# High and low halves of the activations and weights stored woven into one another

## The chip, the core and the metric

The kernel runs on one core of a Trainium2 chip. Five engines matter here: TensorE (PE in the profile, with its loads of the stationary operand shown apart as PEld), VectorE (DVE), ScalarE (ACT), GpSimd (POOL, nearly idle) and SyncE (SP), whose queue issues the transfers. The metric is the device time of one execution in microseconds (us), lower is better.

## What is computed

One decoder layer over 256 tokens of width 4096, in float32: two large products (4096 x 12288 and 4096 x 4096), between them attention over 16 heads and a causal pooling mixer, and around them a modulated normalisation.

```python
c_act = jax.nn.silu(c)
mod = c_act @ w_ada[l] + b_ada[l]
shift, scale, gate = jnp.split(mod, 3, axis=-1)
h = rmsnorm(x, norm_gain[l])
h = h * (1.0 + scale[:, None, :]) + shift[:, None, :]
proj = jnp.einsum('bsd,dn->bsn', h, w_in[l])
q, k, v, g_attn, u_pool, g_pool = jnp.split(proj, ...)
y_attn = longnet_mixture(q, k, v).reshape(B, S, D_ATTN) * jax.nn.silu(g_attn)
y_pool = multiscale_pool(u_pool, w_pool[l], pool_scale[l]) * jax.nn.silu(g_pool)
y = jnp.concatenate([y_attn, y_pool], axis=-1) @ w_out[l]
x = x + gate[:, None, :] * y
return rmsnorm(x, final_gain)
```

## The kernel before

A float32 product is made of three faster ones. Each operand is split into a high half, which ScalarE writes by a cast to the type float32r (4 bytes an element), and a low half, the rounded remainder, which VectorE writes by a subtraction. TensorE then adds high x high, high x low and low x high in PSUM.

Weights come in pieces. `split_piece` (L228) fetches 2 x 128 rows by 512 columns (512 KB) into a tile `raw` (7 buffers), ScalarE casts it into `wh` (L237), VectorE writes the remainder `wl` (L238); `wh` and `wl` have three buffers each. `products` (L241) issues the 12 products of a piece (L248): 2 row tiles x 2 token halves, first the eight that read `wh` as the moving operand (512 columns), against high and low activations in turn, then the four that read `wl`. The stationary operand, 128 x 128, is a token half of the activations: `hh` or `hl` for `w_in`, `yh` or `yl` (tiles named `sa`) for `w_out`.

The activations `hh` and `hl` are made 2 of 32 row tiles at a time by `build_h` (L203): a modulation vector, summed up by VectorE out of `w_ada` (L161), gives scale and bias, ScalarE applies them (`hf`, L221) and casts `hh` (L223), VectorE subtracts to give `hl` (L224). There are 16 such units; five buffers of each tile go round among them (`WIN`).

The work is interleaved by hand: `visit` (L276) walks a chunk of 512 output columns over the activations that are ready, `tick` runs the hooks that make the next modulation vector, and partial sums go to SBUF (L289, L291). The attention and the pooling (`pool_mix`, whose `lin` at L510 reads pieces of `w_pool` as the stationary operand, L522 to L524) run between visits; the gates (L161 on `gacc`) and the chunks of `w_out` (`out_chunk`, L630) come last. The last six pieces of the last chunk are kept in spare tiles so that the second token half can be done apart (L614). Each engine works its queue in program order.

Of the kernel before, what the change touches and what calls it, by code (L numbers as in the profile page):

```python
# [7 lines left out]
F32 = mybir.dt.float32  # L8
F32R = mybir.dt.float32r
AF = mybir.ActivationFunctionType  # L10
ALU = mybir.AluOpType
AX = mybir.AxisListType

P = 128
S = 256
NT = S // P
D = 4096
KT = D // P
CH = 512
# [10 lines left out]
HB = 2  # L30
# [11 lines left out]
PIECE = 2  # L42
# [3 lines left out]
WHB = 3  # L46
WLB = 3
PSB = 2
PSMB = 4
LINE = 512  # L50
RAW = PIECE * CH
# [4 lines left out]
def tile_hybrid_block(  # L56
# [17 lines left out]
    nc = tc.nc  # L74
# [4 lines left out]
    strm = ctx.enter_context(tc.tile_pool(name="strm", bufs=2))  # L79

    def slot_a(shape, dtype=F32):
        return accp.tile(shape, dtype, name="sa", bufs=16, align_bytes=LINE)

    def slot_b(shape, dtype=F32):
        return accp.tile(shape, dtype, name="sb", bufs=8, align_bytes=LINE)
# [4 lines left out]
    def misc():  # L90
        return ps_m.tile([P, CH], F32, name="psm")

    def raw_tile():
        return strm.tile([P, RAW], F32, name="raw", bufs=RAWB)
# [32 lines left out]
    pt = misc()  # L127
# [44 lines left out]
    def flush_work():  # L172
        while delayed:
            delayed.pop(0)()
# [25 lines left out]
    hs = {}  # L200
    htile = {}

    def build_h(u, acc, pool, xT):  # L203
        flush_work()
        uk, k0 = UNITS[u], US[u]
        pc = misc()
        for j in range(2 * uk):
            nc.tensor.matmul(pc[:, j:j + 1], lhsT=acc[:, j * P:(j + 1) * P], rhs=ones, start=True, stop=True)  # L208
        s12 = const.tile([P, 2, HB], F32, name="s12", bufs=2)
        ks = slice(k0, k0 + uk)  # L210
        nc.vector.tensor_tensor(out=s12[:, 0, 0:uk], in0=pc[:, 0:uk], in1=colB[:, ks], op=ALU.add)
        nc.vector.tensor_tensor(out=s12[:, 1, 0:uk], in0=pc[:, uk:2 * uk], in1=gainc[:, ks], op=ALU.mult)
        nc.vector.tensor_tensor(out=s12[:, 1, 0:uk], in0=s12[:, 1, 0:uk], in1=gb[:, ks], op=ALU.add)  # L213
        for a in range(0, uk, 2):
            kk = k0 + a
            if kk % HB == 0:
                htile[kk // HB] = [pool.tile([P, HB, S], F32R, name=n, align_bytes=LINE) for n in ("hh", "hl")]
            hh, hl = [v[:, kk % HB:kk % HB + 2] for v in htile[kk // HB]]
            hf = strm.tile([P, 2, S], F32, name="hf")
            for i in range(2):  # L220
                nc.scalar.activation(out=hf[:, i], in_=xT[:, kk + i], func=AF.Identity,  # L221
                                     scale=s12[:, 1, a + i:a + i + 1], bias=s12[:, 0, a + i:a + i + 1])
            nc.scalar.copy(out=hh, in_=hf)  # L223
            nc.vector.tensor_tensor(out=hl, in0=hf, in1=hh.bitcast(F32), op=ALU.subtract)  # L224
            for i in range(2):
                hs[kk + i] = (hh[:, i], hl[:, i])

    def split_piece(src, n, spare=False):  # L228
        rt = raw_tile()
        v = rt.rearrange("p (k n) -> p k n", n=CH)  # L230
        nc.sync.dma_start(out=v[:, 0:n], in_=src)
        if spare:
            wh, wl = [slot_a([P, PIECE, CH], F32R) for _ in range(2)]
        else:
            wh = strm.tile([P, PIECE, CH], F32R, name="wh", bufs=WHB, align_bytes=LINE)
            wl = strm.tile([P, PIECE, CH], F32R, name="wl", bufs=WLB, align_bytes=LINE)
        nc.scalar.copy(out=wh[:, 0:n], in_=v[:, 0:n])  # L237
        nc.vector.tensor_tensor(out=wl[:, 0:n], in0=v[:, 0:n], in1=wh[:, 0:n].bitcast(F32), op=ALU.subtract)  # L238
        return wh, wl

    def products(pt, hv, wh, wl, first, last):  # L241
        n = len(hv)
        seq = [(t, i, p, wh) for i in range(n) for t in range(NT) for p in range(2)]
        seq += [(t, i, 0, wl) for t in range(NT) for i in range(n)]
        for e, (t, i, p, w) in enumerate(seq):
            started = first and not any(q[0] == t for q in seq[:e])
            ended = last and not any(q[0] == t for q in seq[e + 1:])
            nc.tensor.matmul(pt[t], lhsT=hv[i][p][:, t * P:(t + 1) * P], rhs=w[:, i], start=started, stop=ended)  # L248

    chains = []  # L250
    pending = []
# [2 lines left out]
    def tick(n):  # L254
        for f in hooks:
            f(n)
        for ch in list(chains):
            ch.pop(0)()
            if not ch:
                chains.remove(ch)  # L260
        if pending and len(chains) < DEPTH and not (chains and pending[0][0] == "alone"):
            ch = pending.pop(0)
            if ch[0] == "alone":
                ch.pop(0)
            ch.pop(0)()
            if ch:
                chains.append(ch)
# [76 lines left out]
    for u in range(A0):  # L344
        build_h(u, first[u][0][0], hp, xT)
# [50 lines left out]
    yh = [None] * 8  # L396
    yl = [None] * 8
# [186 lines left out]
    for c, ch in enumerate(order):  # L584
# [5 lines left out]
        elif 12 <= ch < 16:  # L590
            i = ch - 12
# [13 lines left out]
    def need_gate(n):  # L605
        while len(gate_q) > GPS * (7 - n):
            gate_q.pop(0)()

    def prods_of_tile(pt, t, pieces, last):
        seq = []  # L610
        for hv, wh, wl in pieces:
            seq += [(hv[i][p], w[:, i]) for i in range(len(hv)) for p, w in ((0, wh), (1, wh), (0, wl))]
        for e, (h, w) in enumerate(seq):
            nc.tensor.matmul(pt[t], lhsT=h[:, t * P:(t + 1) * P], rhs=w, start=False,  # L614
                             stop=last and e == len(seq) - 1)

    def finish(t, fg):
# [12 lines left out]
    def out_chunk(n):  # L630
        cs = slice(n * CH, (n + 1) * CH)
        if n < 7:
            pw = ps.tile([P, NT, CH], F32, name="mm")
            pt = [pw[:, t] for t in range(NT)]
        else:
            pt = [misc() for t in range(NT)]
        xn.append(slot_b([P, NT, CH]))
        nc.sync.dma_start(out=xn[n], in_=x_v[:, :, cs])
        fg = fin.tile([P, CH], F32, name="fg")
        nc.sync.dma_start(out=fg, in_=fg_v[:, cs].to_broadcast([P, CH]))  # L640
        k = 0
        held = []
        while k < KT:
            m = min(PIECE, KT - k)
            if k + 2 * PIECE >= KT > k + PIECE:
                need_gate(n)
            wh, wl = split_piece(wo_v[:, k:k + m, cs], m, n == 7 and KT - HELD * PIECE <= k < KT - SPARE * PIECE)
            while not all(ydone[kk // HG] == HG for kk in range(k, k + m)):
                tick(0)
            yv = [(yh[kk // 4][:, kk % 4], yl[kk // 4][:, kk % 4]) for kk in range(k, k + m)]  # L650
            if n == 7 and k + m > KT - HELD * PIECE:
                held.append((yv, wh, wl))
                prods_of_tile(pt, 0, held[-1:], k + m == KT)
            else:
                products(pt, yv, wh, wl, k == 0, k + m == KT)
            k += m
            tick(m)
        xc = xn[n]
        gt = gates[n]
        y = fin.tile([P, NT, CH], F32, name="yo")  # L660

        def close(tp):
            w = [P, tp.stop - tp.start, CH]
            src = pw if n < 7 else pt[tp.start].unsqueeze(1)
            nc.vector.tensor_tensor(out=y[:, tp], in0=src, in1=gt.unsqueeze(1).to_broadcast(w), op=ALU.mult)
            nc.vector.tensor_tensor(out=xc[:, tp], in0=y[:, tp], in1=xc[:, tp], op=ALU.add)
            for t in range(tp.start, tp.stop):
                nc.scalar.activation(out=y[:, t], in_=xc[:, t], func=AF.Square, accum_out=ss2[:, t, n:n + 1])

        if n < 7:  # L670
            close(slice(0, NT))
            nc.vector.tensor_tensor(out=xc, in0=xc, in1=fg.unsqueeze(1).to_broadcast([P, NT, CH]), op=ALU.mult)
        else:
            nc.scalar.activation(out=r2, in_=ss2[:, :, 6], func=AF.Sqrt)
            for t in range(NT):
                if t > 0:
                    prods_of_tile(pt, t, held, True)
                close(slice(t, t + 1))
                finish(t, fg)

    for n in range(8):
        out_chunk(n)
# [54 lines left out]
```

## Time and profile before

| | before |
|---|---|
| time, median of 2 runs | 1568.45 us (1568.26 to 1568.64) |
| the profiled execution: its time, its span | 1567.34 us, 1565.4 us |
| PE busy in the span | 1516.3 us, 97% |
| DVE busy | 1405.4 us, 90% |
| ACT busy | 697.6 us, 45% |
| granted TensorE clock | 0.997 of full speed |
| share of PE in the chain that ended last | 91%, 83% in L248 alone |

A group of instructions is read as: line, engine, operation, what it writes and reads, shapes, count, then busy us and mean ns of one, then the idle time of its engine before it and who ended it. Matmuls overlap, so the mean of one is longer than the step from one to the next; the step is read off the start times of a timeline, or from the chain of work, where a stretch of products has its length and its count.

### The profile page before, as it was taken

The numbers are of one execution on the slowest core, as the hardware profiler recorded it, in microseconds if no ns is written. First come the engines' busy times: TensorE is split into PE (matmuls) and PEld (weight loads), VectorE is DVE, ScalarE is ACT, GpSimd is POOL, SyncE is SP. The second block draws the span as 40 slices with busy tenths as digits, with TensorE's granted clock in tenths as the row PEclk, the third lists the DMA queues.
The fourth block names the chain that finished last, engine by engine and source line by source line (L and its number), as shares of the span: only waits on it lengthen the run. The fifth ranks groups of instructions, "written<-read, shape, count | busy, mean of one in ns | idle before, by whom it ended". The sixth has DMA issues, their size and how long they took to land.

```text
span 1565.4 us, 20360 instructions
## 1 busy us (share of the span) xinstructions
PE 1516.3 (97%) x7043; PEld 1257.5 (80%) x7043; DVE 1405.4 (90%) x1759; ACT 697.6 (45%) x820; POOL 0.7 (0%) x5
## 2 busy tenths in 40 slices
PE   2999999999999999999999999999999999999997
PEld 2877888888888888888888888888898888888775
DVE  5988999999999998899999998989988788898886
ACT  4655344443443434344344344556554443444433
POOL 0000000000000000000000000000000000000000
PEclk9999999999999999999999999999999999999999
DMA  9999999999999999899999998867778899998886
GB/s 331 363 335 362 321 331 321 324 308 336 327 310 327 312 330 313 294 326 326 354 340 331 330 333 307 290 226 242 231 250 273 287 357 347 318 339 324 320 305 250
DMA packets 324087, 491.11 MB, mean 314 GB/s; under 512 B 19320, under 2 KB 150664, under 8 KB 323984
## 3 DMA queue, kind: packets, MB, share of 16 engines
q1 hardware_dynamic: 323984, 489.82, 92.2%
q8 instruction: 55, 0.90, 0.2%
q14 instruction: 48, 0.39, 0.1%
HBM read 485.55 MB, written 4.19 MB: 313 GB/s over the span
## 4 chain that ended last, share of the span: by engine, by line
PE 91%; DVE 3%; DMA 3%; issue 1%; ACT 1%; SPq 0%; DVEq 0%; ACTq 0%
PE mm L248 83%; DVE aacc L161 1%; PE psm L614 1%; PE psm L248 1%; DMA raw<-in_w_ada_dram 1%; DMA raw<-in_w_in_dram 1%; PE psm L208 1%; DVE wl L238 1%; ACT wh L237 1%; PE psm L523 0%; PE psm L524 0%; PE psm L522 0%; DMA sb<-in_x_dram 0%; DMA raw<-in_w_out_dram 0%; PE psm L565 0%
## 5 line engine op out<-in xcount | busy, mean ns | idle before, releaser
L237 ACT CAST wh<-raw 128x1024 fp32r<-128x1024 f32 x514 | 538.5, 1050 | 700.0 <-PE mm L248 497.9
L238 DVE TENSOR_TENSOR wl<-raw,wh 128x1024 fp32r<-128x1024 f32 x514 | 624.5, 1218 | 45.1 <-ACT wh L237 41.9
L248 PE MATMUL mm<-wh,hh 128*128 128x512 f32 x1536 | 605.4, 394 | 4.8 <-ACT wh L237 3.8
L248 PE MATMUL mm<-wh,hl 128*128 128x512 f32 x1536 | 599.6, 390 | 0.0
L248 PE MATMUL mm<-wl,hh 128*128 128x512 f32 x1536 | 414.2, 391 | 0.6 <-DVE wl L238 0.6
L161 DVE SCALAR_TENSOR_TENSOR aacc<-raw,cact,aacc 128x512 f32<-128x512 f32 x496 | 371.0, 748 | 31.4 <-DMA raw<-in_w_ada_dram 23.8
L248 PEld LDWEIGHTS mm<-wh,hh 128*128 128x128 f32 x1536 | 288.8, 188 | 67.0 <-ACT wh L237 7.2
L248 PEld LDWEIGHTS mm<-wl,hh 128*128 128x128 f32 x1536 | 288.4, 188 | 61.1 <-DVE wl L238 1.4
L248 PEld LDWEIGHTS mm<-wh,hl 128*128 128x128 f32 x1536 | 288.9, 188 | 58.3 <-issue 0.2
L248 PE MATMUL mm<-wh,sa 128*128 128x512 f32 x896 | 224.0, 392 | 1.9 <-ACT wh L237 1.9
L248 PEld LDWEIGHTS mm<-wh,sa 128*128 128x128 f32 x896 | 167.7, 188 | 39.7 <-ACT wh L237 3.4
L161 DVE SCALAR_TENSOR_TENSOR gacc<-raw,cact,gacc 128x512 f32<-128x512 f32 x248 | 185.5, 748 | 13.5 <-DMA raw<-in_w_ada_dram 9.8
L248 PE MATMUL mm<-wl,sa 128*128 128x512 f32 x448 | 119.8, 389 | 0.0
L291 DVE TENSOR_TENSOR sa<-mm,sa 128x1024 f32<-128x1024 f32 x92 | 112.1, 1218 | 8.5 <-PE mm L248 8.4
L248 PEld LDWEIGHTS mm<-wl,sa 128*128 128x128 f32 x448 | 84.0, 188 | 17.5
L291 DVE TENSOR_TENSOR sb<-mm,sb 128x1024 f32<-128x1024 f32 x48 | 58.5, 1219 | 7.3 <-PE mm L248 7.3
L328 PE MATMUL psm<-diag_r,sb 128*128 128x128 f32 x128 | 16.9, 300 | 15.9 <-DVE diag_r L320 15.9
L221 ACT ACTIVATE hf<-xT,s 128x256 f32<-128x256 f32 x32 | 17.5, 595 | 27.9 <-DVE s L213 27.9
L328 PEld LDWEIGHTS psm<-diag_r,sb 128*128 128x128 f32 x128 | 16.6, 215 | 16.1 <-DVE diag_r L320 16.1
L289 ACT COPY sa<-mm 128x1024 f32<-128x1024 f32 x16 | 16.3, 1016 | 14.2 <-PE mm L248 14.1
L248 PE MATMUL psm<-wh,sa 128*128 128x512 f32 x80 | 20.1, 394 | 1.4 <-ACT wh L237 1.4
L248 PEld LDWEIGHTS psm<-wh,sa 128*128 128x128 f32 x80 | 14.8, 188 | 5.3 <-ACT wh L237 2.2
(113 smaller groups left out, 618.1 us busy)
## 6 DMA issues: line engine op xcount, KB each, us to landing
raw<-in_w_in_dram SPq DMA_DIRECT2D x384, 512.0 KB, 5.7
raw<-in_w_ada_dram SPq DMA_DIRECT2D x512, 256.0 KB, 5.3
raw<-in_w_ada_dram SPq DMA_DIRECT2D x128, 512.0 KB, 6.5
raw<-in_w_out_dram SPq DMA_DIRECT2D x128, 512.0 KB, 6.8
sb<-in_x_dram SPq DMA_DIRECT2D x16, 512.0 KB, 6.4
raw<-in_w_pool_dram SPq DMA_DIRECT2D x8, 512.0 KB, 4.7
out_dram<-sb SPq DMA_DIRECT2D x16, 256.0 KB, 2.6
fg<-in_final_gain_dram SPq DMA_DIRECT2D x8, 256.0 KB, 4.7
```

The lines of the kernel that those rows point to most:

```text
L161: nc.vector.scalar_tensor_tensor(out=acc, in0=r, scalar=cact[:, kt:kt + 1], in1=init if kt == 0 else acc, op0=ALU.mult, op1=ALU.add)
L208: nc.tensor.matmul(pc[:, j:j + 1], lhsT=acc[:, j * P:(j + 1) * P], rhs=ones, start=True, stop=True)
L221: nc.scalar.activation(out=hf[:, i], in_=xT[:, kk + i], func=AF.Identity, scale=s12[:, 1, a + i:a + i + 1], bias=s12[:, 0, a + i:a + i + 1])
L237: nc.scalar.copy(out=wh[:, 0:n], in_=v[:, 0:n])
L238: nc.vector.tensor_tensor(out=wl[:, 0:n], in0=v[:, 0:n], in1=wh[:, 0:n].bitcast(F32), op=ALU.subtract)
L248: nc.tensor.matmul(pt[t], lhsT=hv[i][p][:, t * P:(t + 1) * P], rhs=w[:, i], start=started, stop=ended)
L289: nc.scalar.copy(out=accs[ch], in_=pt)
L291: nc.vector.tensor_tensor(out=accs[ch], in0=pt, in1=accs[ch], op=ALU.add)
L328: nc.tensor.matmul(px[:, i * S + t * P:i * S + (t + 1) * P], lhsT=xs[q][:, t, (2 * a + i) * P:(2 * a + i + 1) * P], rhs=diag_r[:, t], star ...
L614: nc.tensor.matmul(pt[t], lhsT=h[:, t * P:(t + 1) * P], rhs=w, start=False, stop=last and e == len(seq) - 1)
```

## The change

High and low halves get one tile for both. A piece of weights has a tile `wb` of twice the size, with three buffers, in place of `wh` and `wl`. In every other piece the halves lie one behind the other in it, as before; in the rest they are woven: high, low, high, low, so that neighbouring elements of one half are 8 bytes apart where they were 4. The activations of a unit have a tile `hb`, in one of four layouts by turns (`kind`): 0, halves apart (4 bytes between neighbours); 1, high and low woven (8 bytes); 2, both row tiles and both halves woven (16 bytes); 3, halves apart and the two token halves woven (8 bytes between the elements of one token half). The cast and the subtraction of a unit, one instruction each for both row tiles before, are now one for each row tile. `products` and `prods_of_tile` take ready slices, so no product is added, dropped or moved.

```diff
@@ build_h
-                htile[kk // HB] = [pool.tile([P, HB, S], F32R, name=n, align_bytes=LINE) for n in ("hh", "hl")]
-            hh, hl = [v[:, kk % HB:kk % HB + 2] for v in htile[kk // HB]]
+                hb = pool.tile([P, 2 * HB * S], F32R, name="hb", align_bytes=LINE)
+                kind = kk // HB % 4
+                if kind == 0:
+                    v = hb.rearrange("p (l k s) -> p k l s", l=2, k=HB)
+                elif kind == 1:
+                    v = hb.rearrange("p (k s l) -> p k l s", l=2, k=HB)
+                elif kind == 2:
+                    v = hb.rearrange("p (s k l) -> p k l s", l=2, k=HB)
+                else:
+                    v = hb.rearrange("p (k l s t) -> p k l t s", l=2, k=HB, t=NT)
+                htile[kk // HB] = (kind, v)
+            kind, v = htile[kk // HB]
+            hh, hl = [v[:, :, l] for l in range(2)]
...
-            nc.scalar.copy(out=hh, in_=hf)
-            nc.vector.tensor_tensor(out=hl, in0=hf, in1=hh.bitcast(F32), op=ALU.subtract)
+            src = hf if kind < 3 else hf.rearrange("p k (t s) -> p k t s", t=NT)
             for i in range(2):
-                hs[kk + i] = (hh[:, i], hl[:, i])
+                nc.scalar.copy(out=hh[:, i], in_=src[:, i])
+                nc.vector.tensor_tensor(out=hl[:, i], in0=src[:, i], in1=hh[:, i].bitcast(F32), op=ALU.subtract)
+                if kind < 3:
+                    hs[kk + i] = [[q[:, i, t * P:(t + 1) * P] for t in range(NT)] for q in (hh, hl)]
+                else:
+                    hs[kk + i] = [[q[:, i, t] for t in range(NT)] for q in (hh, hl)]
@@ split_piece
-            wh = strm.tile([P, PIECE, CH], F32R, name="wh", bufs=WHB, align_bytes=LINE)
-            wl = strm.tile([P, PIECE, CH], F32R, name="wl", bufs=WLB, align_bytes=LINE)
+            wb = strm.tile([P, 2 * RAW], F32R, name="wb", bufs=WHB, align_bytes=LINE)
+            if count[0] % 2 == 0:
+                wh, wl = [wb[:, l * RAW:(l + 1) * RAW].rearrange("p (k n) -> p k n", n=CH) for l in range(2)]
+            else:
+                wh, wl = [wb.rearrange("p (k n l) -> p l k n", l=2, n=CH)[:, l] for l in range(2)]
+            count[0] += 1
@@ products (prods_of_tile alike, with h[t])
-            nc.tensor.matmul(pt[t], lhsT=hv[i][p][:, t * P:(t + 1) * P], rhs=w[:, i], start=started, stop=ended)
+            nc.tensor.matmul(pt[t], lhsT=hv[i][p][t], rhs=w[:, i], start=started, stop=ended)
```

What each engine waits for changes at one place. On VectorE, in the first half of the program (chunks of `w_in`), the queue of before reads, with the sums of the modulation vector (L161), a partial sum (L291) and the remainders of the weights (L238):

```order
L238 TENSOR_TENSOR wl<-raw,wh 128x1024 [waits DMAHW3_49,Activation_49]
L161 SCALAR_TENSOR_TENSOR aacc<-raw,cact,aacc 128x512 [waits DVE_49]
L238 TENSOR_TENSOR wl<-raw,wh 128x1024 [waits DMAHW6_49,PE_49,Activation_49]
L161 SCALAR_TENSOR_TENSOR aacc<-raw,cact,aacc 128x512 [waits DMAHW7_49,DMAHW0_49,DVE_49]
L161 SCALAR_TENSOR_TENSOR aacc<-raw,cact,aacc 128x512 [waits DVE_49]
L238 TENSOR_TENSOR wl<-raw,wh 128x1024 [waits DMAHW1_49,PE_49,Activation_49]
```

And the same place of the changed program, where L259 is the remainder and `wb` the joint tile:

```order
L259 TENSOR_TENSOR wb<-raw,wb 128x1024 [waits DMAHW3_49,Activation_49]
L161 SCALAR_TENSOR_TENSOR aacc<-raw,cact,aacc 128x512 [waits DMAHW7_49,DMAHW0_49,DVE_49]
L161 SCALAR_TENSOR_TENSOR aacc<-raw,cact,aacc 128x512 [waits DVE_49]
L259 TENSOR_TENSOR wb<-raw,wb 128x1024 [waits DMAHW6_49,Activation_49]
L161 SCALAR_TENSOR_TENSOR aacc<-raw,cact,aacc 128x512 [waits DMAHW4_49,DMAHW3_49,DVE_49]
```

The remainder no longer waits for TensorE; with one tile for both halves, that wait has passed to the cast ahead of it. The cast on ScalarE waited for TensorE before as well, but for the last of the eight products that read `wh`; now it waits for the last of the twelve that read `wb`. Its queue there, before:

```order
L237 CAST wh<-raw 128x1024 [waits DMAHW6_49,DVE_49,PE_49]
L237 CAST wh<-raw 128x1024 [waits DMAHW1_49,DVE_49,PE_49]
L237 CAST wh<-raw 128x1024 [waits DMAHW2_49,DVE_49,PE_49]
L237 CAST wh<-raw 128x1024 [waits DMAHW5_49,DVE_49,PE_49]
L237 CAST wh<-raw 128x1024 [waits DMAHW0_49,DVE_49,PE_49]
```

And in the changed program:

```order
L258 CAST wb<-raw 128x1024 [waits DMAHW6_49,DVE_49,PE_49]
L258 CAST wb<-raw 128x1024 [waits DMAHW1_49,DVE_49,PE_49]
L258 CAST wb<-raw 128x1024 [waits DMAHW2_49,DVE_49,PE_49]
L258 CAST wb<-raw 128x1024 [waits DMAHW5_49,DVE_49,PE_49]
L258 CAST wb<-raw 128x1024 [waits DMAHW0_49,DVE_49,PE_49]
```

The order of the casts and the engines that they wait for are the same; which of TensorE's products they wait for is not in these rows. The products read, at the same place and before:

```order
L248 MATMUL mm<-wh,hh 128x512 [waits Activation_49]
L248 MATMUL mm<-wh,hl 128x512
L248 MATMUL mm<-wh,hh 128x512
L248 MATMUL mm<-wh,hl 128x512
L248 MATMUL mm<-wh,hh 128x512
L248 MATMUL mm<-wh,hl 128x512
L248 MATMUL mm<-wh,hh 128x512
L248 MATMUL mm<-wh,hl 128x512
L248 MATMUL mm<-wl,hh 128x512 [waits DVE_49]
L248 MATMUL mm<-wl,hh 128x512 x3
```

And two pieces of the changed program:

```order
L269 MATMUL mm<-wb,hb 128x512 [waits Activation_49]
L269 MATMUL mm<-wb,hb 128x512 x7
L269 MATMUL mm<-wb,hb 128x512 [waits DVE_49]
L269 MATMUL mm<-wb,hb 128x512 x3
L269 MATMUL mm<-wb,hb 128x512 [waits Activation_49]
L269 MATMUL mm<-wb,hb 128x512 x7
```

The eight products with the high weights still wait for the cast alone, the four with the low ones for the remainder, woven or not: one tile for both halves has not made TensorE wait for both.

## Rows read from the trace of the kernel before

**Rows 1.** The page: busy time, share of the span and count by engine.
```profile
PE 1516.3 (97%) x7043; PEld 1257.5 (80%) x7043; DVE 1405.4 (90%) x1759; ACT 697.6 (45%) x820; POOL 0.7 (0%) x5
```

**Rows 2.** The chain that ended last: shares by line, one stretch (start, length us, count).
```profile
by line: PE mm L248 83.5%; issue 1.2%; DVE aacc L161 1.1%; PE psm L614 1.0%; PE psm L248 0.9%; DMA raw<-in_w_ada_dram 0.8%; DMA raw<-in_w_in_dram 0.8%; PE psm L208 0.7%; DVE wl L238 0.6%; ACT wh L237 0.5%; PE psm L523 0.5%; PE psm L524 0.5%
...
1243.35 57.15 PE mm L248 x252
```

**Rows 3.** Busy time of each engine in four stretches, granted clock, DMA share.
```profile
core 0: us, PE busy (x) PEld busy (x) DVE busy (x) ACT busy (x) POOL busy (x), PEclk, DMA share, GB/s
50.00:150.00 100.00, 96.17 (x416) 76.83 (x415) 88.87 (x110) 60.98 (x65) 0.00 (x0) 0.98 1.04 353
150.00:960.00 810.00, 808.41 (x3617) 670.68 (x3616) 761.45 (x869) 327.76 (x332) 0.53 (x1) 1.00 0.96 323
960.00:1400.00 440.00, 439.41 (x2211) 367.85 (x2210) 391.54 (x577) 215.97 (x285) 0.00 (x0) 1.00 0.85 289
1400.00:1565.40 165.40, 151.13 (x655) 122.01 (x653) 133.00 (x155) 66.61 (x82) 0.00 (x0) 0.98 0.84 304
```

**Rows 4.** Timeline (start us, length us): products of 512 columns and a load.
```profile
800.30 0.39 PE L248 MATMUL mm<-wh,hh 128*128 128x512 f32 x1
800.30 0.19 PEld L248 LDWEIGHTS mm<-wh,hl 128*128 128x128 f32 x1
800.52 0.39 PE L248 MATMUL mm<-wh,hl 128*128 128x512 f32 x1
```

**Rows 5.** Timeline: products of 256 columns in the pooling, and a load.
```profile
1132.31 0.28 PE L524 MATMUL psm<-tq,wl 128*128 128x256 f32 x1
1132.32 0.19 PEld L522 LDWEIGHTS psm<-tq,wh 128*128 128x128 f32 x1
...
1132.43 0.28 PE L522 MATMUL psm<-tq,wh 128*128 128x256 f32 x1
```

**Rows 6.** Groups of instructions by line and shape, whole span.
```profile
L238 DVE TENSOR_TENSOR wl<-raw,wh 128x1024 fp32r<-128x1024 f32 x514 | 624.5, 1218 | 45.1 <-ACT wh L237 41.9
L248 PE MATMUL mm<-wh,hh 128*128 128x512 f32 x1536 | 605.4, 394 | 4.8 <-ACT wh L237 3.8 <-DVE sa L291 1.0
...
L237 ACT CAST wh<-raw 128x1024 fp32r<-128x1024 f32 x514 | 538.5, 1050 | 700.0 <-PE mm L248 497.9 <-DMA raw<-in_w_out_dram 82.1 <-DMA raw<-in_w_in_dram 81.3
...
L224 DVE TENSOR_TENSOR hl<-hf,hh 128x512 fp32r<-128x512 f32 x16 | 10.9, 684 | 0.0
...
L223 ACT CAST hh<-hf 128x512 fp32r<-128x512 f32 x16 | 9.9, 618 | 0.2
...
L565 PE MATMUL psm<-gacc,ones_m 128*128 128x512 f32 x16 | 8.2, 593 | 0.0
...
L530 ACT CAST sa<-y 128x256 fp32r<-128x256 f32 x16 | 6.2, 406 | 13.6 <-DVE y L527 13.6
...
L531 DVE TENSOR_TENSOR sa<-y,sa 128x256 fp32r<-128x256 f32 x16 | 6.1, 419 | 0.2
```

**Rows 7.** Timeline: two casts of weights on ACT, the remainder of the first on DVE.
```profile
799.59 1.05 ACT L237 CAST wh<-raw 128x1024 fp32r<-128x1024 f32 x1 [1.66 <-PE mm L248]
...
801.40 1.22 DVE L238 TENSOR_TENSOR wl<-raw,wh 128x1024 fp32r<-128x1024 f32 x1
...
802.31 1.05 ACT L237 CAST wh<-raw 128x1024 fp32r<-128x1024 f32 x1 [1.67 <-PE mm L248]
```

**Rows 8.** Waits in 150 to 1400 us, of PE alone (total us, times, longest us).
```profile
PE mm L248 <- DVE sa L291: 1.0, 1, 1.0
PE mm L248 <- DVE wl L238: 0.6, 1, 0.6
```

**Rows 9.** Waits in 50 to 150 us.
```profile
PEld mm L248 <- ACT wh L237: 7.2, 10, 2.5
...
PE mm L248 <- ACT wh L237: 3.8, 4, 2.0
```

**Rows 10.** Waits from 1400 us to the end.
```profile
ACT wh L237 <- DMA raw<-in_w_out_dram: 55.0, 34, 5.4
```

More of the change, by code (lines that the diff above doesn't have):

```diff
@@ L222, in build_h @@
                                      scale=s12[:, 1, a + i:a + i + 1], bias=s12[:, 0, a + i:a + i + 1])
-            nc.scalar.copy(out=hh, in_=hf)
-            nc.vector.tensor_tensor(out=hl, in0=hf, in1=hh.bitcast(F32), op=ALU.subtract)
+            src = hf if kind < 3 else hf.rearrange("p k (t s) -> p k t s", t=NT)
             for i in range(2):
-                hs[kk + i] = (hh[:, i], hl[:, i])
+                nc.scalar.copy(out=hh[:, i], in_=src[:, i])
[4 more added lines that the diff above has]
+                    hs[kk + i] = [[q[:, i, t] for t in range(NT)] for q in (hh, hl)]
+    count = [0]
     def split_piece(src, n, spare=False):
@@ L613, in prods_of_tile @@
         for e, (h, w) in enumerate(seq):
-            nc.tensor.matmul(pt[t], lhsT=h[:, t * P:(t + 1) * P], rhs=w, start=False,
+            nc.tensor.matmul(pt[t], lhsT=h[t], rhs=w, start=False,
                              stop=last and e == len(seq) - 1)
@@ L649, in out_chunk @@
                 tick(0)
-            yv = [(yh[kk // 4][:, kk % 4], yl[kk // 4][:, kk % 4]) for kk in range(k, k + m)]
+            yv = [[[q[kk // 4][:, kk % 4, t * P:(t + 1) * P] for t in range(NT)] for q in (yh, yl)]
+                  for kk in range(k, k + m)]
             if n == 7 and k + m > KT - HELD * PIECE:
```

## The prediction

> **What bounds the kernel now.** I read the busy times first: TensorE is busy for 97% of the span, VectorE for 90%, ScalarE for 45% [rows 1]. The chain of work that ended last agrees: 83.5% of it is the products of L248 on TensorE [rows 2]. A busy share alone does not say that TensorE runs at its own pace, so the chain's stretches come next: 252 products took 57.15 us without a break, 0.2268 us each [rows 2]. The timeline shows the same step, 800.30 to 800.52 [rows 4]. The granted clock is 1.00 in the middle of the program [rows 3], that is 2.4 GHz, at which 512 columns are 512 / 2.4 = 0.2133 us. So 94% of a step is the moving operand streaming in, one column a cycle; whatever slows that reading lengthens the step at once. The waits say that nothing else holds TensorE up: from 150 to 1400 us the products of L248 waited 0.6 us for a remainder and 1.0 us for a partial sum, and not once for a cast [rows 8]. Only at the start (50 to 150 us) does it wait for casts, 3.8 us in all [rows 9], and after 1400 us the casts wait for weights, 55.0 us [rows 10], with TensorE busy for 151 of 165 us [rows 3].
>
> **The change, part by part.** Nothing is added to TensorE's queue or taken from it, so the question is the price of spacing. An element is 4 bytes; neighbours that stood 4 bytes apart now stand 8 or 16 apart. No row of the trace has a long read or write with such a step, so each price is bounded.
>
> *Moving operand, 8 bytes.* There are 514 pieces in `wh` and `wl` [rows 6]; every other one is 257, four of them of `w_pool`, where the weights are stationary. That leaves 253 x 12 = 3036 woven moving reads. Below, the price is nothing: still one element a cycle. Above, the nearest row is a product that TensorE takes at a slower pace of reading: with plain float32 operands, 512 columns show 593 ns (L565) against 394 ns (L248) [rows 6], 199 ns more. All of it on each woven read is 3036 x 0.199 = 604 us, half of it 302 us. There is no cover, as the step is 94% streaming. I take nothing: the L565 row is about another operand type, with the same spacing, and says only that a slower pace exists, while two neighbours 8 bytes apart are no more than a skip of one element. This is the choice on which the forecast hangs.
>
> The Trainium skill, SBUF — State Buffer, section Specifications (TRN2), says that a line there has 16 bytes and that full bandwidth needs two or more hits on each line, with a penalty for crossing to a new one. Of a line, a read every 8 bytes takes two float32r elements, so by that rule the woven moving operand is free and the sum is the one below; no run so far shows it.
>
> *Stationary operand, 8 and 16 bytes.* The products with `hh` and `hl` are 3 x 1536 = 4608 (one of the three groups is in [rows 6]); three quarters, 3456, now read woven activations, 1152 of these 16 bytes apart (kind 2). Here there is cover. Products of 256 columns go 0.12 us apart (1132.31 to 1132.43), each with a load of its own, though a load is shown with 0.19 us [rows 5]: a load needs at most 0.12 us of the engine, the rest is latency that overlaps. In the 512-column steps it has 0.2268 us, so 0.107 us is spare, and a load may become 1.9 times as long for nothing. Twice as long is 0.24 - 0.227 = 0.013 us too much: 15 us for kind 2, 45 us if all woven loads paid it. Three times as long is 0.36 - 0.227 = 0.133 us, for kind 2 153 us. I take nothing, since a doubling is nearly covered. A few dozen products of `w_pool` read woven weights as stationary operand without that cover; 96 of them at 0.12 us would be 12 us, and I take nothing there too.
>
> *Casts and remainders of weights.* 257 casts (1050 ns) write and 257 remainders (1218 ns) read and write 8 bytes apart [rows 6]. Below, nothing. Above, I double them. For ScalarE that is 257 x 1.05 = 270 us on 698 us of work in 1565, hidden by its idle time. For VectorE it is 257 x 1.218 = 313 us on 1405.4, which makes 1718 us: more than the span, so VectorE would be the bound. I take nothing: it handles one element of 1024 in 1.19 ns, half TensorE's pace or less, and so asks far less of the memory.
>
> *Activations of a unit.* 16 casts of 618 ns become 32 of about 406 ns, 16 remainders of 684 ns become 32 of about 419 ns (the rows of 128 x 256 at L530 and L531) [rows 6]: +3.1 us on ScalarE, +2.5 us on VectorE over the program. Their idle time hides this, and a unit is made ahead of its use; without that cover it would be 5.6 us. The first row tile of a unit is ready earlier. Zero.
>
> *One tile for both halves.* A cast used to wait for the eight products that read the old `wh`; now it waits for four more, 4 x 0.2268 = 0.91 us. How much lead is there? A cast begins at 799.59 when the eighth product is done, and the next one 2.72 us, that is 12 products, later [rows 7]. With three tiles, its own piece is read after 4 + 24 = 28 products, 6.35 us later. The cast takes 1.05, so it leads by 5.3 us, and by 4.4 after the change. Its remainder began only at 801.40, because VectorE had other work, and took 1.22 [rows 7]; it is due eight products after the piece begins, at 807.75, a lead of 5.1 us. After the change it could begin at 799.59 + 0.91 + 1.05 = 801.55, 0.15 us later than it did. Queued behind the waiting cast are the next casts, the partial sums and the casts of activations; behind the remainder, the sums of L161, which in turn free raw buffers for transfers. All have that lead. It is thin only where TensorE already waits: 3.8 us at the start [rows 9] and a little at the end. Bounds: nothing, and 0.91 us on each of 514 pieces, 466 us, if the lead were all used up. I take +3 us, near the waits that those stages have now.
>
> **Sum.** The profiled execution took 1567.3 us (span 1565.4 and 1.9 around it): 1567.3 + 3 = 1570.3. It was 1.1 us under the median of the runs, so I forecast 1571.5 us.
>
> **The rivals.**
> Moving operand slowed: half of the bound gives 1571.5 + 302 = 1874 us, all of it 2176 us. For it speaks that this read has no cover and its pace is the engine's fastest; against it, that no row shows a cost of spacing. It decides from the first nanosecond: 10.4 ns a woven read are already 2%.
>
> Stationary operand at 16 bytes slowed past its cover: three times as long gives 1571.5 + 153 = 1725 us; twice as long on all woven loads, 1617 us. For it: in kind 2 no two elements of one read are closer than 16 bytes. Against it: 0.107 us of cover in each step [rows 4, 5]. It decides from a load 1.9 times as long. By the rule of the Trainium skill named above (SBUF — State Buffer, Specifications (TRN2)), kind 2 takes a new line for each element and is penalised, with no figure given; the trace of before can neither confirm nor deny it.
>
> VectorE becomes the bound: doubled woven remainders give at least 1718 us, about 1720. For it: 90% busy, with 761 of 810 us in the longest stage [rows 3]. Against it: one element in 1.19 ns is slow work. It decides where a woven remainder grows by some 0.36 us: that stage has 49 us idle and, by its share of the time (810 of the 1515 us from 50 us on), 137 of the 257.
>
> The joint tile eats the lead: if VectorE needs the 0.91 us again and again after bursts, 30 to 60 us, 1600 to 1630 us. It decides where the lead falls under 0.91 us, and outside start and end it is near 5.
>
> Faster: the steps of TensorE would have to shrink, and no product is dropped; only a rearranged wait could give a few us.
>
> **Chances.** Forecast (1562 to 1595 us) 0.60; moving operand slowed wholly 0.14, in part 0.08; stationary operand 0.08; VectorE 0.06; joint tile 0.03; faster 0.01. They follow how much cover each has: none for the moving operand, 0.107 us a step for the stationary one, 49 us for VectorE, nearly 5 us a piece for the joint tile. A measurement of this kernel can tell about 2%, 31 us, from no change; so faster 0.01, same 0.60, slower 0.39. The range goes from 1562 up to 1880: with half of the partly slowed reads in it, 0.60 + 0.04 + 0.08 + 0.06 + 0.03 = 0.81. What it leaves out is mostly the wholly slowed moving read.
>
> **What would show it.** If I am right, products of woven and of plain pieces stand 0.227 us apart, in all four kinds; L258 and L259 keep 1.05 and 1.22 us; casts begin about 0.9 us later against the products that release them, and TensorE's waits between 150 and 1400 us stay at a few us. A step that alternates from piece to piece (12 products and 12 products) shows the moving operand slowed; one that grows for two of eight row tiles, kind 2; a longer mean of L259 with waits of TensorE on it, VectorE; waits of TensorE on casts or remainders with all durations unchanged, the joint tile.

## The result, and the profile after

The changed kernel takes 2264.65 us (2 runs, 2263.68 to 2265.63) against 1568.45 us: 1.4445 times as long, 95% interval 1.4412 to 1.4478. The forecast was 1571.5 us and the range ended at 1880.

The page of the changed kernel, busy times, and of its section on groups the costliest ones (L269 are the products, L258 and L259 the casts and remainders of the weights; columns as in [rows 6]):

```profile
span 2261.9 us, 20379 instructions
...
PE 2215.8 (98%) x7043; PEld 1425.6 (63%) x7043; DVE 1427.4 (63%) x1775; ACT 718.1 (32%) x836; POOL 0.7 (0%) x5
...
L269 PE MATMUL mm<-wb,hb 128*128 128x512 f32 x4608 | 1605.7, 517 | 6.5 <-ACT wb L258 6.5
L269 PEld LDWEIGHTS mm<-wb,hb 128*128 128x128 f32 x4608 | 1012.6, 229 | 559.9 <-issue 396.5
L258 ACT CAST wb<-raw 128x1024 fp32r<-128x1024 f32 x514 | 558.0, 1089 | 1309.4 <-PE mm L269 1146.8
L259 DVE TENSOR_TENSOR wb<-raw,wb 128x1024 fp32r<-128x1024 f32 x514 | 627.6, 1222 | 447.9 <-ACT wb L258 406.5
```

TensorE has as many instructions as before (7043, [rows 1]) and is busy for 700 us more. VectorE and ScalarE have about the work that they had, 1427 and 718 us, and wait for it: casts waited 1146.8 us for products to free their tile. So nobody is late for TensorE; its own products are longer, 517 ns where 394 were shown [rows 6]. The chain of work says it without overlaps (start, length in us, count):

```profile
2063.98 89.90 PE mm L269 x264
```

That is 0.3405 us a product, on average over 22 pieces, every other one woven; before it was 0.2268 [rows 2]. By the start times of the single products in this stretch, the 132 of unwoven pieces are on average 0.230 us apart and the 132 of woven ones 0.452. The timeline of the loads, start and length in us, shows woven steps one by one, since TensorE's loads now stand idle between them:

```profile
1003.24 0.21 PEld L269 LDWEIGHTS mm<-wb,hb 128*128 128x128 f32 x1 [0.25 <-issue]
1003.69 0.21 PEld L269 LDWEIGHTS mm<-wb,hb 128*128 128x128 f32 x1 [0.24 <-issue]
1004.15 3.56 PEld L269 LDWEIGHTS mm<-wb,hb 128*128 128x128 f32 x14 [0.24 <-issue]
...
1007.86 0.31 PEld L269 LDWEIGHTS mm<-wb,hb 128*128 128x128 f32 x1
1008.32 0.31 PEld L269 LDWEIGHTS mm<-wb,hb 128*128 128x128 f32 x1
```

1003.24, 1003.69, 1004.15: 0.45 us apart. At 1007.86 the activations are of kind 2 (16 bytes apart): their loads show 0.31 us instead of 0.19 to 0.21, and yet the step is 0.46. Waiting is not the cause: between 150 and 1900 us the products of L269 waited once, for 2.0 us.

```profile
PE mm L269 <- ACT wb L258: 2.0, 1, 2.0
```

### The profile page after: what moved, and what is told of

Its sections match the earlier page's. It is cut to its first block, busy times and chain, and to the rows that moved or that the text cites. A ratio compares the mean times of both kernels' runs of the same rounds, so it can differ in the third digit from the quotient of the medians.

```text
span 2261.9 us, 20379 instructions
## 1 busy us (share of the span) xinstructions
PE 2215.8 (98%) x7043; PEld 1425.6 (63%) x7043; DVE 1427.4 (63%) x1775; ACT 718.1 (32%) x836; POOL 0.7 (0%) x5
## 4 chain that ended last, share of the span: by engine, by line
PE 92%; DVE 0%; ACT 0%; DVEq 0%; issue 0%; ACTq 0%
PE mm L269 85%; PE psm L269 2%; PE psm L635 1%; PE psm L208 0%; PE psm L544 0%; PE psm L545 0%; PE psm L543 0%; PE psm L432 0%; PE psm L456 0%; PE psm L586 0%; PE psm L473 0%; PE psm L480 0%; PE psm L522 0%; PE psm L511 0%; PE psm L455 0%; PE psm L481 0%
## 5 line engine op out<-in xcount | busy, mean ns | idle before, releaser
L269 PE MATMUL mm<-wb,hb 128*128 128x512 f32 x4608 | 1605.7, 517 | 6.5 <-ACT wb L258 6.5
L269 PEld LDWEIGHTS mm<-wb,hb 128*128 128x128 f32 x4608 | 1012.6, 229 | 559.9 <-issue 396.5
L258 ACT CAST wb<-raw 128x1024 fp32r<-128x1024 f32 x514 | 558.0, 1089 | 1309.4 <-PE mm L269 1146.8
L259 DVE TENSOR_TENSOR wb<-raw,wb 128x1024 fp32r<-128x1024 f32 x514 | 627.6, 1222 | 447.9 <-ACT wb L258 406.5
L269 PE MATMUL mm<-wb,sa 128*128 128x512 f32 x1344 | 461.3, 513 | 0.0
L269 PEld LDWEIGHTS mm<-wb,sa 128*128 128x128 f32 x1344 | 265.2, 197 | 192.7 <-issue 165.1
L161 DVE SCALAR_TENSOR_TENSOR aacc<-raw,cact,aacc 128x512 f32<-128x512 f32 x496 | 371.1, 748 | 15.2 <-DMA raw<-in_w_ada_dram 8.1
L312 DVE TENSOR_TENSOR sa<-mm,sa 128x1024 f32<-128x1024 f32 x92 | 112.5, 1222 | 146.6 <-PE mm L269 146.5
L161 DVE SCALAR_TENSOR_TENSOR gacc<-raw,cact,gacc 128x512 f32<-128x512 f32 x248 | 185.6, 748 | 5.2 <-DMA raw<-in_w_ada_dram 1.6
L269 PE MATMUL psm<-wb,sa 128*128 128x512 f32 x120 | 41.0, 511 | 0.0
L269 PEld LDWEIGHTS psm<-wb,sa 128*128 128x128 f32 x120 | 23.7, 198 | 17.2 <-issue 14.5
L208 PEld LDWEIGHTS psm<-ones,aacc 128*128 128x128 f32 x128 | 16.9, 193 | 4.6 <-issue 3.9
L161 DVE SCALAR_TENSOR_TENSOR gacc<-raw,cact,bz 128x512 f32<-128x512 f32 x8 | 6.0, 750 | 19.5 <-PE psm L586 19.4
L544 PE MATMUL psm<-tq,wb 128*128 128x256 f32 x64 | 18.1, 283 | 0.0
```

The source lines that it names most:

```text
L161: nc.vector.scalar_tensor_tensor(out=acc, in0=r, scalar=cact[:, kt:kt + 1], in1=init if kt == 0 else acc, op0=ALU.mult, op1=ALU.add)
L269: nc.tensor.matmul(pt[t], lhsT=hv[i][p][t], rhs=w[:, i], start=started, stop=ended)
L312: nc.vector.tensor_tensor(out=accs[ch], in0=pt, in1=accs[ch], op=ALU.add)
L544: nc.tensor.matmul(o, lhsT=wh, rhs=pl, start=False, stop=False)
```

## The experiments

**Which part.** The first theory after the result: a moving operand read at 8-byte spacing goes at half the pace, and that is nearly all of the loss. Rivals: the stationary operand has a large share, or the slow pace needs both operands woven. Three kernels take the parts asunder. In the first, weights are never woven (the tile is still joint):

```diff
-            if count[0] % 2 == 0:
+            if True:
```

> The weights stay unwoven in the joint tile, the activations keep their four layouts. In the changed kernel a product with unwoven weights follows the one before by 0.227 us where the activations are unwoven, 0.230 where neighbours are 8 bytes apart and 0.237 where they are 16 apart. If the woven moving operand alone makes the loss and the stationary one costs what these steps show, the time is 1568 + 2304 x 0.0035 + 1152 x 0.0095 = about 1587 us. If the stationary operand costs nothing by itself, 1568 to 1572. If it took a good part of the 696 us, over 1700.

Measured: 1594.75 us, 1.0168 times before (1.0141 to 1.0195). The second weaves weights alone:

```diff
-                kind = kk // HB % 4
+                kind = 0
```

> Every unit of activations unwoven, every other piece of weights woven as in the changed kernel. If the woven moving operand makes the loss, 3036 products go from 0.2268 to about 0.452 us apart and the time is 1568 + 3036 x 0.225 = about 2251 us. If the loss needs both operands woven (the load and the stream reading spread lines at the same time), products with woven weights would be less than 0.40 us apart and the time under 2100.

Measured: 2250.47 us, 1.4357 times before (1.4325 to 1.4388). The chain has the same stretch as the changed kernel:

```profile
2050.10 89.90 PE mm L269 x264
```

The third has both edits, so nothing is woven:

> Nothing is woven; what is left is the joint tile of a piece and the casts and remainders of a unit by row tile. If the joint tile's later release of 0.91 us is covered, 1566 to 1575 us, the same as before within 0.4%. If the lead is used up in places, 1580 to 1630 us, with TensorE waiting for casts and remainders between 150 and 1400 us.

Measured: 1572.09 us, 1.0023 times before (1.0011 to 1.0034): 4.8 us more than the 1567.28 of before in these runs. Its waits of TensorE, all program (us, times, longest), answer to the casts in [rows 9]:

```profile
PE mm L269 <- ACT wb L258: 8.2, 4, 2.2
...
PE mm L269 <- DVE wb L259: 1.2, 4, 0.5
```

So the weave of the weights costs 2250.47 - 1572.09 = 678 us, 0.2235 us on each of 3036 products; that of the activations 1594.75 - 1572.09 = 22.7 us; the joint tile with the divided casts 4.8 us. The first two were taken one without the other; together they cost 692.6 us (2264.65 - 1572.09), a little less than their sum of 701.

**Why half pace.** Four theories of the moving read. Fetches are of 8 bytes, and a lone element wastes half of one. Or any gap in the stream costs. Or it is the type float32r. Or what counts is how many elements are taken of one 16-byte line in a row. Layouts of the woven pieces tell them apart; activations are unwoven in all that follow but one. Of each edit only the lines of the layout are shown; left out are those that bring the source of the cast and the output of the product into the same shape, and where `w_pool` is kept unwoven. Each kernel from here to the part on the stationary operand was timed once. First, high and low by turns after every two elements (`j=2`), then after every four (`j=4`); in both, pieces of `w_pool` stay unwoven:

```diff
-                wh, wl = [wb.rearrange("p (k n l) -> p l k n", l=2, n=CH)[:, l] for l in range(2)]
+                wh, wl = [wb.rearrange("p (k n l j) -> p l k n j", l=2, k=PIECE, j=2)[:, l] for l in range(2)]
```

> Activations unwoven; in every other piece of weights (those of the pooling excepted) high and low change places after every two elements: high, high, low, low. A high half is then read in runs of 8 bytes, 16 bytes from run to run: half of each 16 bytes is read, as in the woven layout, but neighbours come in twos. If the stream is fetched 8 bytes at a time and a lone element wastes half a fetch, products with such weights go 0.227 us apart and the time is about 1570 us. If it is the number of 16-byte lines that counts (two elements read of each, as when woven), they stay at 0.452 us and the time is about 2250. If any gap in the stream costs, also 2250.

> As the kernel with pairs, but high and low change places after every four elements: runs of 16 bytes, 32 from run to run, each run one aligned line of 16 bytes. The bytes in use are half of the stretch, as before. If what counts is how many 16-byte lines the stream touches, 512 columns touch 128 lines as unwoven weights do: steps of 0.227 us and about 1572 us. If any gap in the stream halves its pace, 0.452 us and about 2250 us.

Measured: 2250.8 us with runs of two, 1589.18 with runs of four. The chain of either, twos first:

```profile
2051.09 89.90 PE mm L271 x264
```

```profile
1319.66 60.94 PE mm L271 x264
```

Runs of two go exactly as single elements do, 0.452 us by the start times: 8-byte fetches are out. Runs of four leave a gap after each, and by the start times in that stretch they go 0.231 us apart, the unwoven pieces between them 0.230: a gap as such is not it. The 17 us over the kernel that weaves nothing do not lie on the woven products alone: over the program the steps of pieces in runs of four add up to 10.6 us more than the same pieces there, those of unwoven pieces to 5.6 us more. The cause of both stays open.

Then the type. The products take the upper two bytes of both operands as bfloat16 (the lower bits, with all that they add, are left out):

```diff
-            nc.tensor.matmul(pt[t], lhsT=hv[i][p][t], rhs=w[:, i], start=started, stop=ended)
+            nc.tensor.matmul(pt[t], lhsT=top(hv[i][p][t]), rhs=top(w[:, i]), start=started, stop=ended)
```

> The weave of the weights and plain activations as in the kernel with plain activations, but the products of L248 take only the upper two bytes of each element, as bfloat16, of both operands: this leaves out the lower bits, the low products included. Neighbours of a moving operand are then 2-byte elements 4 bytes apart in the unwoven pieces (a gap after each, 128 lines of 16 bytes) and 8 bytes apart in the woven ones (256 lines). If lines count, unwoven pieces go about 0.22 to 0.23 us apart and woven ones about 0.43 to 0.45, about 2250 us in all. If any gap halves the pace, both go at 0.43 to 0.45, about 2900 us. If it is a matter of the type float32r, neither is slowed: under 1600.

Measured: 2239.52 us.

```profile
2040.46 89.54 PE mm L272 x264
```

0.339 us on average, as with float32r. The loads show which pieces are slow:

```profile
1000.60 2.82 PEld L272 LDWEIGHTS <-hb 128*128 128x128 bf16 x13 [0.34 <-issue]
1003.75 0.12 PEld L272 LDWEIGHTS <-hb 128*128 128x128 bf16 x1 [0.34 <-issue]
1004.20 0.12 PEld L272 LDWEIGHTS <-hb 128*128 128x128 bf16 x1 [0.34 <-issue]
```

The thirteen steps from 1000.60 to 1003.75 take 3.15 us: one woven step of 0.45 and the twelve of an unwoven piece, 0.225 each. So unwoven pieces, with a 2-byte gap after each 2-byte element, are not slowed; woven ones, 8 bytes apart, are. In the unwoven pieces half of each line's bytes is left out, as in the woven float32r ones, but four elements come from a line and not two. So what counts is how many elements come from a line, not their type, and not the share of its bytes that is used. Last, high weights in runs of four that begin in the middle of a line (the low ones in runs of two, two elements of each line):

```diff
+                h4 = wb.rearrange("p (x e) -> p x e", e=8)[:, :, 2:6]
+                l4 = wb.rearrange("p (x a b) -> p x a b", a=4, b=2)[:, :, 0::3]
```

> Activations unwoven. In every other piece of weights (those of the pooling excepted) the layout repeats every 32 bytes: two low elements, four high, two low. A high run of four begins in the middle of a 16-byte line and ends in the middle of the next, so that a stream takes two elements of each line, one after the other, though the runs are as long as in the kernel with runs of four; low elements come in two runs of two, two of each line. If it is the elements taken of one line in a row that set the pace, all 3036 products go 0.45 us apart: about 2250 us. If it is the length of the runs, wherever they begin, the 2024 high ones go 0.23 us apart and the 1012 low ones 0.45: about 1800 us. If runs of two are fast when two of them lie close together, under 1650.

Measured: 2250.1 us.

```profile
2050.40 89.90 PE mm L282 x264
```

The same runs of four, moved by 8 bytes, are at half pace, 0.452 us by the start times. So the 16-byte line decides, and two elements taken of it are not enough. Three are the next question, in bfloat16 again, for the high weights only (one place in four empty, 510 columns instead of 512):

```diff
+                h3 = wb[:, RAW:RAW + 1360].rearrange("p (k x e) -> p k x e", k=2, e=4)[:, :, :, 0:3]
+                l3 = wb[:, 0:RAW].rearrange("p (k n) -> p k n", n=CH)[:, :, 0:510]
```

> Products of L248 in bfloat16 on the upper two bytes of both operands (the lower bits are left out), activations unwoven. In every other piece but the first of a visit the high weights stand in runs of three in a line of 16 bytes, the fourth place empty, and the low ones are unwoven; such products have 510 columns, so two columns of 512 are left out there. Six of seven raw buffers are kept. About 1536 products read runs of three. The bfloat16 kernel with woven pieces came to 2239 us, with unwoven products 0.225 us apart and woven ones 0.453; without woven ones that is about 1550 us. If fewer than four elements of a line in a row halve the pace, 0.45 us and about 1900 us. If a line takes four cycles of the stream whatever is read of it, three columns in four cycles, 0.297 us and about 1660. If three are enough, 0.225 and about 1550.

Measured: 1674.15 us. The loads before such products, one step each:

```profile
805.20 0.10 PEld L282 LDWEIGHTS <-hb 128*128 128x128 bf16 x1 [0.20 <-issue]
805.50 0.10 PEld L282 LDWEIGHTS <-hb 128*128 128x128 bf16 x1 [0.20 <-issue]
805.80 0.10 PEld L282 LDWEIGHTS <-hb 128*128 128x128 bf16 x1 [0.20 <-issue]
806.10 0.10 PEld L282 LDWEIGHTS <-hb 128*128 128x128 bf16 x1 [0.20 <-issue]
```

0.300 us: 170 lines at four cycles of 2.4 GHz are 0.283, and 0.013 us a product were there before (0.2268 against 0.2133). Three columns in four cycles, as the line theory had it.

**One element of a line.** That theory also had a line cost four cycles whatever is taken of it. The test: both row tiles and both halves woven, 16 bytes between neighbours.

```diff
+                wh, wl = [wb.rearrange("p (n k l) -> p l k n", l=2, n=CH)[:, l] for l in range(2)]
```

> Activations unwoven; in every other piece both row tiles and both halves of the weights are woven, so that neighbours of a moving operand are 16 bytes apart, each in a line of its own. If the stream gets one line in four cycles, 512 lines take four times the unwoven 128: steps of about 4 x 0.213 + 0.013 to 4 x 0.2268, that is 0.87 to 0.91 us, and about 1572 + 3036 x 0.66 = 3580 us. If a gap in the stream halves its pace and no more, 0.452 us and about 2250 us.

Measured: 2295.3 us, not 3580: here the theory fell. The stretch of the chain, and the casts and remainders:

```profile
L259 DVE TENSOR_TENSOR wb<-raw,wb 128x1024 fp32r<-128x1024 f32 x514 | 852.1, 1659 | 414.4 <-ACT wb L258 360.8 <-DMA raw<-in_w_ada_dram 47.8 <-DMA raw<-in_w_in_dram 5.3
L258 ACT CAST wb<-raw 128x1024 fp32r<-128x1024 f32 x514 | 812.9, 1587 | 1112.2 <-PE mm L269 1016.8 <-issue 42.8 <-DMA raw<-in_w_out_dram 18.9
```

```profile
2093.16 91.17 PE mm L269 x264
```

By the start times a woven step is 0.460 us (an unwoven one 0.232): one element of each line goes at two cycles a column, hardly slower than two of each. Is that because neighbouring lines are fetched ahead? Two kernels use every second line only, with one element of it (`j=2`, the stream passes twice over the stretch) or two (`e=2`):

```diff
+                wh, wl = [wb.rearrange("p (x j k l) -> p l k j x", l=2, k=PIECE, j=2)[:, l] for l in range(2)]
```

```diff
+                wh, wl = [wb.rearrange("p (x k l e) -> p l k x e", l=2, k=PIECE, e=2)[:, l] for l in range(2)]
```

> Activations unwoven; in every other piece of weights (those of the pooling excepted) neighbours of a moving operand are 32 bytes apart: one element of every second 16-byte line, the stream passing over the stretch twice. With one element of every line (16 bytes apart) the step was 0.460 us, two cycles a column. If an element read alone costs two cycles wherever the next one lies, 0.46 us again, about 2300 us, or a little more for the slower casts and remainders. If two cycles a column held only because lines in a row were fetched ahead, and a line otherwise takes four, 0.87 us and about 3550 us.

> Activations unwoven; in every other piece of weights (those of the pooling excepted) a moving operand is read in runs of two, 32 bytes from run to run: two elements of every second line. Runs of two, 16 bytes from run to run, went 0.452 us apart. If a line of which two elements are taken costs four cycles wherever the next line lies, 0.452 us and about 2250 us; if skipping lines costs extra, more than 0.5 us; if the four cycles came of neighbouring lines getting in each other's way, less than 0.40 us and under 2100 us.

Measured: 2191.0 and 2277.48 us. Chains, single elements first:

```profile
1996.77 87.03 PE mm L271 x264
```

```profile
2075.66 91.01 PE mm L271 x264
```

By the start times, 0.430 and 0.460 us a woven product. The distance of the lines hardly matters; a skipped line makes a single element even a little cheaper. What the stream takes, by what it takes of a line (a step is read from start times; cycles are of 2.4 GHz, the granted clock being 1.00 in these stretches, and leave out the 0.003 to 0.033 us that a product takes beyond them):

| elements of a 16-byte line in a row | step, us | cycles a column | cycles a line |
|---|---|---|---|
| 4 (unwoven) | 0.2268 | 1 | 4 |
| 4 (runs of four) | 0.231 | 1 | 4 |
| 3 | 0.300 | 1.33 | 4 |
| 2 (woven, pairs, or runs that cross) | 0.452 | 2 | 4 |
| 2, every second line | 0.460 | 2 | 4 |
| 1, every line | 0.460 | 2 | 2 |
| 1, every second line | 0.430 | 2 | 2 |

That a line costs four cycles from two elements on, and two for one, is what was measured; why a second element costs two more and a third and fourth none stays open.

**The stationary operand.** All units in kind 2, weights unwoven:

```diff
-                kind = kk // HB % 4
+                kind = 2
```

> Weights unwoven, the activations of all units in the layout with 16 bytes between neighbours. With the activations in four layouts, such products went 0.236 us apart and their loads showed 310 ns, unwoven ones 0.227 and 188. If each product pays this for itself, 4608 x 0.0095 = 44 us over the kernel that weaves nothing (1572), about 1616 us. If the load can be hidden but for the change from one layout to another, under 1590. If a longer load builds up behind itself, over 1650.

Measured: 1610.78 us, 1.0273 times before (1.0250 to 1.0295).

```profile
L269 PEld LDWEIGHTS mm<-wb,hb 128*128 128x128 f32 x4608 | 1091.3, 310 | 10.6 <-ACT wb L258 7.8 <-ACT sm L464 0.2
```

Loads show 310 ns instead of 188, 122 ns more, and the time grew by 1610.78 - 1572.09 = 38.7 us over the kernel that weaves nothing, 8.4 ns a product. A load at 16-byte spacing is shown 1.65 times as long, and most of that is covered by the product before. But the price does not follow the length of the load. In the kernel with woven activations and unwoven weights, the chain has a stretch in which most loads are of activations 8 bytes apart, and one of the `w_out` part, where the stationary operand is not woven:

```profile
859.03 61.34 PE mm L269 x264
...
1330.06 59.87 PE mm L269 x264
```

That is 0.2323 and 0.2268 us a product. By the start times in that kernel, products whose load shows 188 ns mostly go 0.227 us apart, those with 193 ns (8 bytes) 0.232 to 0.233, those with 310 ns (16 bytes) 0.233. A load only 5 ns longer costs nearly as much as one 122 ns longer; why a woven stationary operand costs these 5 to 8 ns stays open.

## Why the prediction was wrong, point by point

**What bounds the kernel** was right, and was the reason why the loss is so large: TensorE's step is 94% streaming, TensorE waits for hardly anything, and what slows the stream lengthens the span at once.

**The moving operand** is the step that failed: "I take nothing". It named the read without cover and the 3036 products, both right, and then took the lower end of the price. The price is 0.2235 us, 678 us in all. The reason given, that 8 bytes are "no more than a skip of one element", was an argument without a row; the experiments show that taking two elements of a 16-byte line where there were four halves the pace, whether by single elements, pairs or runs that cross. The rival "moving operand slowed" had the mechanism, with 0.14 for the full price, and even that was too small: 2176 us against 2265. Its sign, a step that alternates from piece to piece, is what the trace shows (0.230 and 0.452 us). Its 199 ns came from mean durations of overlapping products (593 and 394 ns). The trace of before has two of the slower products in a row:

```profile
1041.92 1.02 PE L565 MATMUL psm<-gacc,ones_m 128*128 128x512 f32 x2
```

The second starts at 1041.92 + 1.02 - 0.593 = 1042.35, so the step is 0.43 us, 0.206 more than 0.2268 by the start times (0.433): 626 us on 3036 products, and 2198 us for the rival. That would have been the better bound, but still too small: woven, the step nearly doubles, 0.2268 to 0.452. The range ended at 1880 because the fully slowed read was what it left out.

The sentence of the Trainium skill weighed there (SBUF — State Buffer, section Specifications (TRN2)) asks for two or more hits on a 16-byte line for full bandwidth. The line is borne out as the unit; for TensorE's moving read the number is not: two hits gave 0.452 us, three 0.300, four 0.2268. The measurement decides. The penalty that it names for a new line at each element shows in the loads of kind 2, 310 ns against 188.

**The stationary operand**: taken at nothing, measured 22.7 us. The cover held for long loads (122 ns longer at 16 bytes left 8.4 ns to see), but the sum looked for a price only where a load outgrows its cover, and loads just 5 ns longer cost 5 to 6 ns a product as well. No row of before could show that price. The rival of a tripled load did not come: with 122 ns more on the 0.12 us that the prediction gave a load, it doubled, an estimate from these two rows.

**Casts and remainders**: right at 8 bytes, nearly. The mean of 1089 ns over half woven casts makes a woven one 2 x 1089 - 1050 = 1128 ns, 78 more, on an engine that is idle for two thirds of the span; remainders hardly change (2 x 1222 - 1218 = 1226 for a woven one). The doubling set as an upper end came only at 16 bytes: 2 x 1587 - 1050 = 2124 ns and 2 x 1659 - 1218 = 2100 ns in the kernel with 16-byte steps. There VectorE did not become the bound, since TensorE's span had grown past it.

**Activations of a unit**: 406 and 419 ns were forecast, means of 469 and 471 came:

```profile
L237 DVE TENSOR_TENSOR hb<-hf,hb 128x256 fp32r<-128x256 f32 x32 | 13.7, 471 | 1.1 <-ACT hb L236 1.1
L236 ACT CAST hb<-hf 128x256 fp32r<-128x256 f32 x32 | 13.0, 469 | 0.0
```

With all units in kind 2 they were 663 and 639 ns, so a quarter of them at that length explains the means. Off the path, as said.

**The joint tile**: +3 us forecast, 4.8 measured together with the divided casts, and in part where it was said to be: products waited 8.2 us for casts, against 5.8 before, of these 6.5 us between 50 and 150 us, where it was 3.8 [rows 9], and none between 150 and 1400 us. What makes up the rest of the 4.8 us is not shown.

## What to carry to other kernels

Lay the moving operand of a product out so that four elements in a row come from one aligned 16-byte line; if float32r halves must share a tile, let them change places after 16 bytes, which cost 1.1% here (1589 us beside 1572), where every other weave of the two halves of the weights cost 39% or more. The stationary operand and the operands of casts stood neighbours 8 bytes apart well: about 6 ns a product, and 78 ns a cast and 8 ns a remainder on engines with idle time. And where a read has no cover and no row gives its price, the upper end deserves as much of the chance as the lower, above all if the engine is at its full pace already.

## What the runs showed of the hardware that was not expected

Two float32r elements of a 16-byte line cost as much of TensorE's stream as four (0.452 us for 512 columns at two of a line, 0.2268 at four), even when they are neighbours; bfloat16 elements 4 bytes apart, four to a line, go at full pace (0.225 us). A single element of a line goes hardly slower than two, 0.460 us, and 0.430 if every second line is skipped. A stationary operand woven at 8 or 16 bytes adds 5 to 8 ns to a step of 227 ns, though its loads are shown 5 and 122 ns longer. Writing woven weights, ScalarE's casts and VectorE's remainders (which also read a woven operand) go at nearly full pace with neighbours 8 bytes apart (1128 and 1226 ns for 1024 elements, against 1050 and 1218) and at about half pace with 16 (2124 and 2100 ns).
